# A two-layer encoder trunk on one core: the second layer's compressed rows normalised and turned for all token tiles together

## The chip, the cores and the metric

The kernel runs on one core of a Trainium2 chip. The metric is the device time of one execution in microseconds (us); the median of several runs is given. A core has five engines with a queue of instructions each: TensorE (PE in the profile, with its weight loads as PEld), VectorE (DVE), ScalarE (ACT), GpSimd (POOL) and SyncE (SP), which here issues the DMAs. Each engine works through its queue in order; semaphores make it wait for others.

## The reference

Two layers over 512 tokens of width 1024, in float32. Layer 0 is neighbourhood attention; layer 1, which the change touches, is multi-head latent attention with 16 heads:

```python
def mixer_mla(xn, w_in, q_norm, w_qb, kv_norm, w_kvb, w_out):
    c_q, c_kv, k_rope, z = jnp.split(xn @ w_in, [384, 384 + 256, 384 + 256 + 32], axis=-1)
    q = (rmsnorm(c_q, q_norm) @ w_qb).reshape(B, S, H, 64 + 32)
    q_nope, q_pe = jnp.split(q, [64], axis=-1);  q_pe = apply_rope(q_pe, cos, sin)
    kv = (rmsnorm(c_kv, kv_norm) @ w_kvb).reshape(B, S, H, 64 + 64)
    k_nope, v = jnp.split(kv, [64], axis=-1)
    k_pe = apply_rope(k_rope[:, :, None, :], cos, sin)      # one rotary key for all heads
    k = concat([k_nope, broadcast(k_pe)]);  q = concat([q_nope, q_pe])
    o = block_attention(q, k, v)                            # dense, softmax over 512 keys
    return (o.reshape(B, S, H * 64) * silu(z)) @ w_out
```

Each layer ends with an output projection, a residual add and a gated per-layer embedding; one RMS norm closes the trunk.

## The kernel before

Tokens lie in four tiles of 128 (NT = 4). Every float32 operand of a matmul is split into a rounded part (hi) and its remainder (lo), and a product is made of three matmuls: hi by hi, lo by hi, hi by lo. `load_w` (line 67) fetches a weight tile by a DMA on SP, ACT makes hi (line 76) and POOL makes lo (line 77); three buffers each. `split` (line 81) does the same for a result in PSUM: ACT copies hi (line 83), DVE subtracts (line 85, or 87 with a scale). `mms` (line 93) issues a chain of matmuls (line 96). PSUM has eight banks: two named mm, two named S, three named T for transposes and one named O.

The order of each engine's queue is not the order of the program's lines. The kernel is built with a planner that keeps a model of the engines' time: among the instructions that it holds ready, it takes the earliest in program order, and so lays out every queue ahead. `issue_after(ins)` adds that what is traced inside it on the engine of `ins` comes after `ins` in that engine's queue.

Layer 1, up to the attention, is done in these steps:

- **Compression (`mla_c`, line 408).** The 672 columns c_q (384), c_kv (256) and the rotary key (32) are computed in two parts, of 384 and of 288 columns. In each part all four token tiles take 24 matmuls (names ps_mm and ps_S), and ACT copies the result into the tile's own rows `c` (line 423). Then, tile by tile: `rms` of c_q and c_kv into one buffer `cn` of 768 columns (ACT squares with a sum, line 104; DVE forms the mean, line 105; POOL takes the power -1/2, line 106; DVE scales, line 111); the rotary key by four products (lines 436 to 439) into `tp` and sums (lines 441, 442) into two places of `cn`, whose other columns are cleared (lines 434, 435); six transposes (line 122), of which five blocks are split into `cT` and the sixth into the slabs `slab_h` and `slab_l`.
- **Rotary rows.** Two sets of query and key tiles (`sets`: qe, qo, ke, ko, hi and lo each) serve the head pairs in turn. Twelve DMAs (`move`, line 90) take the rotary key's rows from the slabs to ke, ko and, as zeros, to qo of both sets.
- **Heads (`mla_heads`).** `z_phase` computes seven of eight gates z (24 matmuls each, activation in line 152). `group(g)` (line 477), for four heads, computes the rotary queries (ACT copy, line 483; a shuffle and products, lines 484 to 487; hi and lo, lines 490 and 491) and then the values: for each token tile six matmuls into 256 columns of an mm bank, which `v_split` (line 174) splits into a tile `vt`. `project(j)` (line 507), for a pair of heads, computes queries and keys into two mm banks, splits the halves into the set of j, and moves the rotary queries by four DMAs. `attend(j)` (line 527) runs two heads (`mla_head`): for each of four query tiles three score matmuls into a bank S, a row maximum (DVE, line 559), the exponential with a sum (ACT, line 561), a division (DVE and POOL, lines 562 and 563), four transposes and a split; then eight matmuls into O.

```python
        zs = self.z_phase(a["mla_z"], xT, range(NEARLY))
        group(0)
        last = project(0)
        zs.update(self.z_phase(a["mla_z"], xT, range(NEARLY, 8)))
        for j in range(8):
            if j < 7 and j % 2 == 1:
                group((j + 1) // 2)
            attend(j)
            if j < 7:
                last = project(j + 1)
```

Of the kernel before, what the change touches and what calls it, by code (L numbers as in the profile page):

```python
# [13 lines left out]
F32 = mybir.dt.float32  # L14
F32R = mybir.dt.float32r
AF = mybir.ActivationFunctionType
# [3 lines left out]
P = 128  # L20
# [12 lines left out]
def win(t, r0, r1, off, dims):  # L33

    b = t[r0:r1]
    return bass.AP(tensor=b.tensor, offset=b.offset + off, ap=[list(b.ap[0])] + [list(d) for d in dims])


class Trunk:
# [52 lines left out]
    def mms(self, out, terms):  # L92
        nc = self.nc
        n = len(terms)
        for i, (l, r) in enumerate(terms):
            last = nc.tensor.matmul(out, l, r, start=i == 0, stop=i == n - 1)  # L96
        return last
# [76 lines left out]
    def v_split(self, vt, ps):  # L174

        src = ps.rearrange("p (g e c) -> p g e c", g=2, e=2)
        hi = win(vt, 0, P, 0, [[256, 2], [192, 2], [1, 64]])
        lo = win(vt, 0, P, 64, [[256, 2], [64, 2], [1, 64]])
        self.split(hi, lo, src)
# [228 lines left out]
    def mla_c(self, pool, xT, cT, sets):  # L408
# [5 lines left out]
        cs = [pool.tile([P, 672], F32, name=f"c{t}", tag="c", bufs=4) for t in range(NT)]  # L414
        xh, xl = xT
        L = lambda s, k, t: s[k // 4][:, k % 4, t * P:(t + 1) * P]
        for part, (w0, wn) in enumerate(((0, 384), (384, 288))):
            ws = [self.load_w(a["mla_c"][part][c], 2 * wn, extra=c == 3) for c in range(4)]
            for t in range(NT):
                ps = self.psum("S" if part == 0 and t >= 2 else "mm")  # L420
                W = lambda s, k: ws[k // 2][s][:, (k % 2) * wn:(k % 2 + 1) * wn]
                self.mms(ps[:, :wn], self.by_chunk(lambda s, k: L(xT[s], k, t), W))
                nc.scalar.activation(cs[t][:, w0:w0 + wn], ps[:, :wn], AF.Copy)
        slab_h = pool.tile([P, S], F32R, name="slab_h", tag="slab", bufs=2)
        slab_l = pool.tile([P, S], F32R, name="slab_l", tag="slab", bufs=2)
        for t in range(NT):
            c = cs[t]
            cn = pool.tile([P, 768], F32, name="cn", tag="cn", bufs=1)
            self.rms(cn[:, 0:384], c[:, 0:384], gq, 384)
            self.rms(cn[:, 384:640], c[:, 384:640], gkv, 256)  # L430
            cos, sin = tok[:, t, 0, :], tok[:, t, 1, :]
            x1, x2 = c[:, 640:656], c[:, 656:672]
            tp = pool.tile([P, 64], F32, name="tp", tag="tp", bufs=2)
            nc.vector.memset(cn[:, 640:672], 0.0)
            nc.vector.memset(cn[:, 736:768], 0.0)
            nc.vector.tensor_tensor(out=tp[:, 0:16], in0=x1, in1=cos, op=ALU.mult)
            nc.vector.tensor_tensor(out=tp[:, 16:32], in0=x2, in1=sin, op=ALU.mult)
            nc.vector.tensor_tensor(out=tp[:, 32:48], in0=x1, in1=sin, op=ALU.mult)
            nc.vector.tensor_tensor(out=tp[:, 48:64], in0=x2, in1=cos, op=ALU.mult)
            for b in (672, 704):  # L440
                nc.vector.tensor_tensor(out=cn[:, b:b + 16], in0=tp[:, 0:16], in1=tp[:, 16:32], op=ALU.subtract)
                nc.vector.tensor_tensor(out=cn[:, b + 16:b + 32], in0=tp[:, 32:48], in1=tp[:, 48:64], op=ALU.add)
            t1 = self.transposes([cn[:, i * P:(i + 1) * P] for i in range(4)])
            self.split(cT[0][:, 0:4, t * P:(t + 1) * P], cT[1][:, 0:4, t * P:(t + 1) * P],
                       t1.rearrange("p (a b) -> p a b", a=4))
            t2 = self.transposes([cn[:, i * P:(i + 1) * P] for i in range(4, 6)])
            self.split(cT[0][:, 4, t * P:(t + 1) * P], cT[1][:, 4, t * P:(t + 1) * P], t2[:, 0:P])
            self.split(slab_h[:, t * P:(t + 1) * P], slab_l[:, t * P:(t + 1) * P], t2[:, P:2 * P])
        for st in sets:
            for s, sl in enumerate((slab_h, slab_l)):  # L450
                self.move(st["ke"][s][64:96], sl[64:96])
                self.move(st["ko"][s][0:64], sl[0:64])
                self.move(st["qo"][s][0:32], sl[0:32])

    def mla_heads(self, pool, xT, cT, sets, oT):
# [21 lines left out]
        def group(g):  # L477
# [293 lines left out]
```

## Time and profile before

| | |
|---|---|
| median of 3 runs | 690.96 us (690.71 to 692.72) |
| the profiled execution's own time | 690.26 us |
| its span, first to last instruction | 688.5 us |
| TensorE's granted clock | 0.998 |
| busy: PE, PEld, DVE, ACT, POOL | 664.4, 566.9, 356.3, 402.1, 396.7 us |
| HBM traffic over the span | 107 GB/s |

A row of the profile names the line of the kernel, the engine, the operation, and the tiles as out<-in, then shapes, count and times. In a timeline a row begins with its start and its length in us; neighbours of one kind are merged (x8 is eight of them), and brackets give the engine's idle time just before and what ended it. The lengths of neighbouring matmuls overlap. In the table by stretches each engine has its busy time in that stretch. The rows of a tile give the least, the middle and the greatest length in ns.

### The profile page before, as it was taken

Reading aid. Unit: us, or ns where it says so; the run is one execution under the profiler, and the core shown is the slowest. Engines: PE = TensorE matmul, PEld = TensorE weight load, DVE = VectorE, ACT = ScalarE, POOL = GpSimd, SP = SyncE. Lnnn points to the kernel's source line nnn. Section 1 sums busy time; section 2 is a strip of 40 time slices with the busy share of each in tenths; the row PEclk is TensorE's granted clock in tenths of the full one; section 3 lists DMA queues with packets and bytes.
Section 4 is the critical chain, followed back from the end, with each engine's and each line's share of the span. In section 5 each row is a group of like instructions: output and inputs, shape, how many; then the busy total and the mean of one; then the engine's idle time right before and its main releaser. Section 6 shows DMA issues by size and latency. Waiting matters only on the chain.

```text
span 688.5 us, 10118 instructions
## 1 busy us (share of the span) xinstructions
PE 664.4 (97%) x3580; PEld 566.9 (82%) x3580; DVE 356.3 (52%) x813; ACT 402.1 (58%) x799; POOL 396.7 (58%) x309
## 2 busy tenths in 40 slices
PE   5999999999999999999999998999999999999995
PEld 4789898998988888788899886787888777887885
DVE  4300364647737624633524503788988886055333
ACT  6722576666767562643443634878888878426433
POOL 1753557467575565853044634777789867658511
PEclk9999999999999999999999999999999999999999
DMA  8731423323223127544243344203121201584122
GB/s 324 234 121 62 133 86 104 105 72 97 85 92 108 40 97 301 167 130 135 89 104 107 107 121 116 81 23 93 24 70 37 86 1 68 191 308 154 61 77 92
DMA packets 28642, 77.53 MB, mean 113 GB/s; under 512 B 3632, under 2 KB 6704, under 8 KB 28592
## 3 DMA queue, kind: packets, MB, share of 16 engines
q1 hardware_dynamic: 28592, 76.89, 33.9%
q8 instruction: 28, 0.46, 0.3%
q14 instruction: 22, 0.18, 0.1%
HBM read 65.34 MB, written 8.39 MB: 107 GB/s over the span
## 4 chain that ended last, share of the span: by engine, by line
PE 86%; ACT 5%; DVE 4%; issue 2%; DMA 1%; POOL 1%; SPq 0%; POOLq 0%; DVEq 0%; ACTq 0%
PE ps_mm L96 63%; PE ps_S L96 9%; PE ps_T L122 5%; PE ps_O L96 4%; PE ps_O L335 2%; PE ps_T L323 1%; ACT ex L561 1%; ACT whi L76 1%; DMA x<-x 1%; PE ps_S L288 1%; PE ps_S L287 1%; DVE mx L559 1%; POOL wlo L77 0%; DVE mx L301 0%; ACT pt_hi L83 0%
## 5 line engine op out<-in xcount | busy, mean ns | idle before, releaser
L77 POOL TENSOR_TENSOR wlo<-wraw,whi 128x1024 fp32r<-128x1024 f32 (+3 forms) x96 | 218.3, 2287 | 118.5 <-ACT whi L76 68.4
L76 ACT ACTIVATE whi<-wraw 128x1024 fp32r<-128x1024 f32 (+4 forms) x100 | 97.9, 988 | 97.0 <-PE ps_mm L96 32.1
L563 POOL TENSOR_TENSOR ex<-ex,rc 128x512 f32<-128x512 f32 x64 | 66.2, 1048 | 20.7 <-DVE rc L562 13.9
L96 PE MATMUL ps_mm<-whi,hnT 128*128 128x512 f32 (+1 forms) x272 | 69.7, 377 | 0.0
L96 PEld LDWEIGHTS ps_mm<-whi,hnT 128*128 128x128 f32 x272 | 49.5, 188 | 9.5
L310 POOL TENSOR_TENSOR ex<-ex,rc 128x128 f32<-128x128 f32 (+1 forms) x64 | 34.3, 560 | 38.1 <-DVE rc L306 36.5
L559 DVE TENSOR_REDUCE mx<-ps_S 128x1 f32<-128x512 f32 x64 | 43.7, 685 | 15.3 <-PE ps_S L96 14.3
L96 PE MATMUL ps_mm<-xh,whi 128*128 128x512 f32 x192 | 50.9, 398 | 0.1
L96 PE MATMUL ps_mm<-xh,wlo 128*128 128x512 f32 x192 | 49.1, 391 | 0.0
L561 ACT ACTIVATE ex<-ps_S,mx 128x512 f32<-128x512 f32 x64 | 44.1, 689 | 8.2 <-DVE mx L559 6.7
L96 PE MATMUL ps_mm<-xl,whi 128*128 128x512 f32 x192 | 48.6, 392 | 0.0
L85 DVE TENSOR_TENSOR pt_lo<-ps_T,pt_hi 128x512 fp32r<-128x512 f32 x64 | 43.0, 679 | 5.0 <-ACT pt_hi L83 4.6
L305 ACT ACTIVATE ex<-ex,mx 128x128 f32<-128x128 f32 (+1 forms) x64 | 30.2, 473 | 22.0 <-DVE mx L301 21.6
L106 POOL TENSOR_TENSOR rs<-ss,half 128x1 f32<-128x1 f32 x24 | 13.0, 549 | 50.3 <-DVE ss L105 49.0
L96 PEld LDWEIGHTS ps_mm<-xl,whi 128*128 128x128 f32 x192 | 35.6, 188 | 7.3
L96 PEld LDWEIGHTS ps_mm<-xh,wlo 128*128 128x128 f32 x192 | 35.6, 188 | 7.0
L83 ACT ACTIVATE pt_hi<-ps_T 128x512 fp32r<-128x512 f32 x64 | 37.0, 597 | 7.6 <-PE ps_T L122 7.3
L96 PE MATMUL ps_mm<-wlo,hnT 128*128 128x512 f32 (+1 forms) x136 | 40.6, 379 | 0.0
L96 PEld LDWEIGHTS ps_mm<-xh,whi 128*128 128x128 f32 x192 | 34.5, 188 | 6.4 <-ACT z L152 0.4
L122 PE MATMUL ps_T<-ident,ex 128*128 128x128 f32 x256 | 36.3, 273 | 0.2 <-DVE pt_lo L85 0.2
L122 PEld LDWEIGHTS ps_T<-ident,ex 128*128 128x128 f32 x256 | 30.7, 141 | 6.8 <-issue 0.7
L85 DVE TENSOR_TENSOR vt<-ps_mm,vt 128x256 fp32r<-128x256 f32 x32 | 13.2, 415 | 44.3 <-ACT vt L83 44.0
(215 smaller groups left out, 1579.7 us busy)
## 6 DMA issues: line engine op xcount, KB each, us to landing
pe<-pe SPq DMA_DIRECT2D x32, 256.0 KB, 2.9
wraw<-na_qk SPq DMA_DIRECT2D x16, 512.0 KB, 3.4
wraw<-gate SPq DMA_DIRECT2D x16, 512.0 KB, 3.4
wraw<-na_z SPq DMA_DIRECT2D x8, 512.0 KB, 4.2
wraw<-na_v SPq DMA_DIRECT2D x8, 512.0 KB, 3.3
wraw<-na_o SPq DMA_DIRECT2D x8, 512.0 KB, 3.4
wraw<-mla_z SPq DMA_DIRECT2D x8, 512.0 KB, 4.2
wraw<-mla_o SPq DMA_DIRECT2D x8, 512.0 KB, 3.6
```

Source lines behind the costliest of these rows:

```text
L76: nc.scalar.activation(hi[:, c], raw[:, c], AF.Copy)
L77: (rest or nc.gpsimd).tensor_tensor(out=lo[:, c], in0=raw[:, c], in1=hi[:, c].bitcast(F32), op=ALU.subtract)
L83: nc.scalar.activation(hi, src, AF.Copy, scale=scale)
L85: nc.vector.tensor_tensor(out=lo, in0=src, in1=hi.bitcast(F32), op=ALU.subtract)
L96: last = nc.tensor.matmul(out, l, r, start=i == 0, stop=i == n - 1)
L122: self.nc.tensor.transpose(t[:, i * P:(i + 1) * P], b, self.ident)
L305: self.last_exp = nc.scalar.activation(e, e, AF.Exp, bias=mx[:, qt:qt + 1], accum_out=sm[:, qt:qt + 1])
L310: nc.gpsimd.tensor_tensor(out=e, in0=e, in1=rc[:, qt:qt + 1].to_broadcast([P, e.shape[1]]), op=ALU.mult)
L335: nc.tensor.matmul(O[:, o:o + w], vh[kt], s[:, c:c + w], start=n == 0, stop=n == 7, skip_group_check=True)
L559: nc.vector.reduce_max(mx[:, c], sp, axis=AX.X, negate=True)
L561: nc.scalar.activation(ex, sp, AF.Exp, bias=mx[:, c], accum_out=sm[:, c])
L563: nc.gpsimd.tensor_tensor(out=ex, in0=ex, in1=rc[:, c].to_broadcast([P, S]), op=ALU.mult)
```

## The change

- In `mla_c` the four tiles' rows are one buffer `c` of 128 x 4 x 672. The squares are taken by ACT straight from PSUM, behind the copy, with the sums in one tile `ss` of eight columns. POOL forms mean and power for four tiles at once, in each part; DVE scales the rows in place. The rotary key of all four tiles is computed in eight wide instructions into a cleared tile `kr`. The transposes of all tiles come behind that.
- Only the first set gets its rotary rows from the slabs (six DMAs). The second set's six are copied from the first set, traced after `project(0)`.
- In `group` two token tiles share one mm bank: twelve matmuls, and one split of 512 columns into a `vt` of twice the width.
- `mms` notes its last matmul, and `attend(0)` is traced under `issue_after` of the eighth gate's last matmul.

```diff
@@ -411,46 +412,50 @@
         nc.sync.dma_start(tok, a["rope_tok"])
         gq = self.bcast(pool, a["q_norm"], 384, "gq")
         gkv = self.bcast(pool, a["kv_norm"], 256, "gkv")
-        cs = [pool.tile([P, 672], F32, name=f"c{t}", tag="c", bufs=4) for t in range(NT)]
+        c = pool.tile([P, NT, 672], F32, name="c", tag="c", bufs=1)
+        ss = pool.tile([P, 2 * NT], F32, name="ssc", tag="ssc", bufs=1)
         xh, xl = xT
         L = lambda s, k, t: s[k // 4][:, k % 4, t * P:(t + 1) * P]
-        for part, (w0, wn) in enumerate(((0, 384), (384, 288))):
-            ws = [self.load_w(a["mla_c"][part][c], 2 * wn, extra=c == 3) for c in range(4)]
+
+        for part, (w0, wn, n, g) in enumerate(((0, 384, 384, gq), (384, 288, 256, gkv))):
+            ws = [self.load_w(a["mla_c"][part][k], 2 * wn, extra=k == 3) for k in range(4)]
             for t in range(NT):
                 ps = self.psum("S" if part == 0 and t >= 2 else "mm")
                 W = lambda s, k: ws[k // 2][s][:, (k % 2) * wn:(k % 2 + 1) * wn]
                 self.mms(ps[:, :wn], self.by_chunk(lambda s, k: L(xT[s], k, t), W))
-                nc.scalar.activation(cs[t][:, w0:w0 + wn], ps[:, :wn], AF.Copy)
+                nc.scalar.activation(c[:, t, w0:w0 + wn], ps[:, :wn], AF.Copy)
+                sq = pool.tile([P, 384], F32, name="sqc", tag="sqc", bufs=1)
+                nc.scalar.activation(sq[:, :n], ps[:, :n], AF.Square, accum_out=ss[:, part * NT + t:part * NT + t + 1])
+            r = ss[:, part * NT:(part + 1) * NT]
+            nc.gpsimd.tensor_scalar(r, r, 1.0 / n, EPS, op0=ALU.mult, op1=ALU.add)
+            nc.gpsimd.tensor_tensor(out=r, in0=r, in1=self.half.to_broadcast([P, NT]), op=ALU.pow)
+            for t in range(NT):
+                v = c[:, t, w0:w0 + n]
+                nc.vector.scalar_tensor_tensor(v, v, ss[:, part * NT + t:part * NT + t + 1], g, op0=ALU.mult, op1=ALU.mult)
+
+        kr = pool.tile([P, NT, P], F32, name="kr", tag="kr", bufs=1)
+        nc.gpsimd.memset(kr, 0.0)
+        tp = pool.tile([P, 4, NT, 16], F32, name="tp", tag="tp", bufs=1)
+        x1, x2 = c[:, :, 640:656], c[:, :, 656:672]
+        cos, sin = tok[:, :, 0, :], tok[:, :, 1, :]
+        for i, (x, f) in enumerate(((x1, cos), (x2, sin), (x1, sin), (x2, cos))):
+            nc.vector.tensor_tensor(out=tp[:, i], in0=x, in1=f, op=ALU.mult)
+        for b in (32, 64):
+            nc.vector.tensor_tensor(out=kr[:, :, b:b + 16], in0=tp[:, 0], in1=tp[:, 1], op=ALU.subtract)
+            nc.vector.tensor_tensor(out=kr[:, :, b + 16:b + 32], in0=tp[:, 2], in1=tp[:, 3], op=ALU.add)
         slab_h = pool.tile([P, S], F32R, name="slab_h", tag="slab", bufs=2)
         slab_l = pool.tile([P, S], F32R, name="slab_l", tag="slab", bufs=2)
         for t in range(NT):
-            c = cs[t]
-            cn = pool.tile([P, 768], F32, name="cn", tag="cn", bufs=1)
-            self.rms(cn[:, 0:384], c[:, 0:384], gq, 384)
-            self.rms(cn[:, 384:640], c[:, 384:640], gkv, 256)
-            cos, sin = tok[:, t, 0, :], tok[:, t, 1, :]
-            x1, x2 = c[:, 640:656], c[:, 656:672]
-            tp = pool.tile([P, 64], F32, name="tp", tag="tp", bufs=2)
-            nc.vector.memset(cn[:, 640:672], 0.0)
-            nc.vector.memset(cn[:, 736:768], 0.0)
-            nc.vector.tensor_tensor(out=tp[:, 0:16], in0=x1, in1=cos, op=ALU.mult)
-            nc.vector.tensor_tensor(out=tp[:, 16:32], in0=x2, in1=sin, op=ALU.mult)
-            nc.vector.tensor_tensor(out=tp[:, 32:48], in0=x1, in1=sin, op=ALU.mult)
-            nc.vector.tensor_tensor(out=tp[:, 48:64], in0=x2, in1=cos, op=ALU.mult)
-            for b in (672, 704):
-                nc.vector.tensor_tensor(out=cn[:, b:b + 16], in0=tp[:, 0:16], in1=tp[:, 16:32], op=ALU.subtract)
-                nc.vector.tensor_tensor(out=cn[:, b + 16:b + 32], in0=tp[:, 32:48], in1=tp[:, 48:64], op=ALU.add)
-            t1 = self.transposes([cn[:, i * P:(i + 1) * P] for i in range(4)])
+            t1 = self.transposes([c[:, t, i * P:(i + 1) * P] for i in range(4)])
             self.split(cT[0][:, 0:4, t * P:(t + 1) * P], cT[1][:, 0:4, t * P:(t + 1) * P],
                        t1.rearrange("p (a b) -> p a b", a=4))
-            t2 = self.transposes([cn[:, i * P:(i + 1) * P] for i in range(4, 6)])
+            t2 = self.transposes([c[:, t, 4 * P:5 * P], kr[:, t, :]])
             self.split(cT[0][:, 4, t * P:(t + 1) * P], cT[1][:, 4, t * P:(t + 1) * P], t2[:, 0:P])
             self.split(slab_h[:, t * P:(t + 1) * P], slab_l[:, t * P:(t + 1) * P], t2[:, P:2 * P])
-        for st in sets:
-            for s, sl in enumerate((slab_h, slab_l)):
-                self.move(st["ke"][s][64:96], sl[64:96])
-                self.move(st["ko"][s][0:64], sl[0:64])
-                self.move(st["qo"][s][0:32], sl[0:32])
+        for s, sl in enumerate((slab_h, slab_l)):
+            self.move(sets[0]["ke"][s][64:96], sl[64:96])
+            self.move(sets[0]["ko"][s][0:64], sl[0:64])
+            self.move(sets[0]["qo"][s][0:32], sl[0:32])
 
     def mla_heads(self, pool, xT, cT, sets, oT):
         nc, a = self.nc, self.a
@@ -492,15 +497,17 @@
             R[g] = rh, rl
             wkv = self.load_w(a["mla_kv"][g], 1024)
             vts = []
-            for t in range(NT):
+            for t0 in range(0, NT, 2):
                 ps = self.psum("mm")
-                L = lambda s, k: cT[s][:, 3 + k, t * P:(t + 1) * P]
                 W = lambda s, k: wkv[s][:, 512 + k * 256:512 + (k + 1) * 256]
-                self.mms(ps[:, :256], [(L(0, k), W(0, k)) for k in range(2)] + [(L(1, k), W(0, k)) for k in range(2)]
-                         + [(L(0, k), W(1, k)) for k in range(2)])
-                vt = pool.tile([P, S], F32R, name="vt", tag="vt", bufs=8)
-                self.v_split(vt, ps[:, :256])
-                vts.append(vt)
+                for t in (t0, t0 + 1):
+                    L = lambda s, k: cT[s][:, 3 + k, t * P:(t + 1) * P]
+                    self.mms(ps[:, (t - t0) * 256:(t - t0 + 1) * 256],
+                             [(L(0, k), W(0, k)) for k in range(2)] + [(L(1, k), W(0, k)) for k in range(2)]
+                             + [(L(0, k), W(1, k)) for k in range(2)])
+                vt = pool.tile([P, 2 * S], F32R, name="vt", tag="vt", bufs=4)
+                self.v_split(vt, ps)
+                vts += [vt[:, :S], vt[:, S:]]
             V[g] = vts
             W_[g] = wkv, self.load_w(a["mla_qn"][g], 768)
 
@@ -535,11 +542,16 @@
         zs = self.z_phase(a["mla_z"], xT, range(NEARLY))
         group(0)
         last = project(0)
+        for s in range(2):
+            for n, r in (("ke", slice(64, 96)), ("ko", slice(0, 64)), ("qo", slice(0, 32))):
+                self.move(sets[1][n][s][r], sets[0][n][s][r])
         zs.update(self.z_phase(a["mla_z"], xT, range(NEARLY, 8)))
+        first = self.last_mm.ins
         for j in range(8):
             if j < 7 and j % 2 == 1:
                 group((j + 1) // 2)
-            attend(j)
+            with self.tc.issue_after(first) if j == 0 else nullcontext():
+                attend(j)
             if j < 7:
                 last = project(j + 1)
         return last.ins
```

`v_split` takes the number of groups of 128 columns from the shape of its bank (`g = ps.shape[1] // 128`) where it had 2.

More of the change, by code (lines that the diff above doesn't have):

```diff
@@ L95, in mms @@
         for i, (l, r) in enumerate(terms):
-            last = nc.tensor.matmul(out, l, r, start=i == 0, stop=i == n - 1)
+            last = self.last_mm = nc.tensor.matmul(out, l, r, start=i == 0, stop=i == n - 1)
         return last
@@ L174, in v_split @@
     def v_split(self, vt, ps):
-        src = ps.rearrange("p (g e c) -> p g e c", g=2, e=2)
-        hi = win(vt, 0, P, 0, [[256, 2], [192, 2], [1, 64]])
-        lo = win(vt, 0, P, 64, [[256, 2], [64, 2], [1, 64]])
+        g = ps.shape[1] // 128
+        src = ps.rearrange("p (g e c) -> p g e c", g=g, e=2)
+        hi = win(vt, 0, P, 0, [[256, g], [192, 2], [1, 64]])
+        lo = win(vt, 0, P, 64, [[256, g], [64, 2], [1, 64]])
         self.split(hi, lo, src)
```

## The prediction

> **What bounds the kernel now.** I read the page first: its engine line and the chain of waits by engine.
>
> ```profile
> span 688.5 us, 10118 instructions
> PE 664.4 (97%) x3580; PEld 566.9 (82%) x3580; DVE 356.3 (52%) x813; ACT 402.1 (58%) x799; POOL 396.7 (58%) x309
> ...
> PE 86%; ACT 5%; DVE 4%; issue 2%; DMA 1%; POOL 1%; SPq 0%; POOLq 0%; DVEq 0%; ACTq 0%
> ```
>
> TensorE (PE) is busy 664.4 of 688.5 us and owns 86% of the chain. The diff adds and removes no matmul and no transpose: the value products keep their 24 matmuls per group, the 24 turns of compressed rows stay 24. So the time can move only through PE's idle time, 24.1 us in all, and only through that part of it that lies where the edits act. The table by stretches (columns: PE, PEld, DVE, ACT, POOL busy with counts, clock, DMA) and the list of what PE waited for between 340 and 480 us show how little that is:
>
> ```profile
> 350.00:360.00 10.00, 9.42 (x56) 8.85 (x55) 1.29 (x2) 5.69 (x11) 7.09 (x5) 1.00 0.40 109
> 410.00:420.00 10.00, 8.79 (x48) 7.31 (x47) 3.15 (x6) 4.03 (x7) 6.26 (x5) 1.00 0.74 215
> 420.00:430.00 10.00, 9.23 (x39) 6.75 (x38) 3.11 (x5) 3.78 (x7) 2.42 (x2) 1.00 0.25 68
> 430.00:440.00 10.00, 8.68 (x42) 6.96 (x41) 5.35 (x11) 8.68 (x17) 6.68 (x5) 1.00 0.15 34
> ```
>
> ```profile
> PE ps_S L96 <- ACT ex L561: 2.5, 2, 1.3
> PE ps_mm L96 <- DVE vt L85: 0.8, 1, 0.8
> PE ps_S L96 <- ACT ke L83: 0.7, 1, 0.7
> PE ps_mm L96 <- ACT c L423: 0.6, 1, 0.6
> PE ps_mm L96 <- ACT xr L483: 0.3, 1, 0.3
> ```
>
> 0.58 us is idle at the seam of the two compression parts (350 to 360), 1.21, 0.77 and 1.32 us between 410 and 440, where the first value products, the first head pair's projection and the eighth gate lie. The five waits add to 4.9 us. That is the stake: well under 1% of the span.
>
> **Squares from PSUM.** Rows of ACT and PE at the seam, and the squares of now:
>
> ```profile
> 358.77 0.85 ACT L423 ACTIVATE c<-ps_mm 128x384 f32<-128x384 f32 x2
> ...
> 359.30 0.53 PE L96 MATMUL ps_mm<-whi,x1h 128*128 128x288 f32 x2 [0.58 <-ACT c L423]
> ...
> L104 ACT ACTIVATE cn<-c x8: 417/477/536, 359.9 to 393.7; 128x384 f32<-128x384 f32 x4, 128x256 f32<-128x256 f32 x4
> L104 ACT ACTIVATION_READ_ACCUMULATOR cn<-c x8: 187/204/212, 360.3 to 394.0; 128x1 f32 x8
> ```
>
> Part two's first matmul waits 0.58 us for a bank that the copy of c empties. The eight squares stay eight, but now they read the bank too, so it is held for one more ACT instruction and its accumulator read: at most 0.54 + 0.20 us, less what the two overlap by. I take +0.5 us. The ends are 0 (the other tile's bank is freed first) and +1.1 (both copies of 0.42 us and a square go ahead of the release). At the other tiles 24 matmuls lie between a bank's uses, and nothing waits.
>
> **Normalising and turning together.** Eight powers on POOL become two (each with a small multiply-add that DVE did eight times), and a clearing of 512 columns is added there; on DVE 32 rope instructions of 16 columns become eight of 64 (strided, over the four tiles), and eight clearings go. The eight scalings stay, in place. All of part two's work now starts behind the last compressed tile. What covers it is the gate phase (z):
>
> ```profile
> 372.69 2.10 PE L96 MATMUL ps_mm<-x1h,whi 128*128 128x512 f32 x8
> ...
> 412.96 1.52 PE L96 MATMUL ps_mm<-cT,whi 128*128 128x512 f32 x6
> ```
>
> From 372.69 to 412.96 us PE runs seven gates without a wait, and the first reader of the turned rows comes behind them. So I cost this edit at 0, as PE's order is written ahead and can put the 24 turns anywhere in those 40 us. What it costs if a turn stands too early is a rival below.
>
> **Six of twelve moves later.** On SP's queue:
>
> ```profile
> 402.30 0.60 SPq L90 DMA_DIRECT2D ke<-slab_h  x1
> ...
> 409.99 0.53 SPq L75 DMA_DIRECT2D wraw<-mla_z  x1
> ...
> 421.84 0.51 SPq L90 DMA_DIRECT2D qe<-rh  x1
> ...
> 414.57 1.06 ACT L76 ACTIVATE whi<-wraw 128x1024 fp32r<-128x1024 f32 x1 [0.81 <-PE ps_mm L96]
> ```
>
> The twelve moves hold SP from 402.30 us to the fetch of the eighth gate's weights at 409.99, 0.64 us each. Six fewer would fetch these 3.8 us earlier, but ACT's conversion of them waits for PE, not for the transfer, so nothing is won. The six later copies take the same 3.8 us of SP. They are traced past the four rope moves of the first pair and ahead of the eighth gate's load. That load is traced behind the rope moves now as well, and the queue has it 12 us ahead of them (409.99 against 421.84), since it waits for nothing; the copies' source rows, too, are long in place by then. So both can go early, and the copies at worst put the load back to where it is now. Cost 0; the upper end, a load held back by some copies until its conversion is late, is +1.
>
> **Values, two tiles to a bank.**
>
> ```profile
> 416.16 0.74 PE L96 MATMUL ps_mm<-whi,cT 128*128 128x256 f32 x4 [0.29 <-ACT xr L483]
> ...
> 419.03 0.74 PE L96 MATMUL ps_mm<-whi,cT 128*128 128x256 f32 x4 [0.79 <-DVE vt L85]
> ...
> 417.12 1.52 DVE L485 TENSOR_TENSOR xr<-xr,rope_c 128x512 f32<-128x512 f32 x1
> ...
> L83 ACT ACTIVATE vt<-ps_mm x32: 360/383/410, 56.9 to 529.1; 128x256 fp32r<-128x256 f32 x32
> ```
>
> Now four banks are asked for, of two. Tile two waits 0.29 us for the bank of the rotary queries, tile four 0.79 us, since the rest of tile two stood on DVE behind a rotary product that took 1.52 us. With two tiles to a bank both waits lie inside a bank: the first pair keeps PE busy until the rotary bank is free, and the second pair takes that one. I take -1.1 us, the two waits. The ends are -1.2 (all idle time of that stretch) and -0.4: the rest of pair one can fall behind the same 1.52 us, and then the query projection waits for it.
>
> **The eighth gate ahead of the first scores.**
>
> ```profile
> 422.81 0.61 PE L96 MATMUL ps_mm<-cT,wlo 128*128 128x512 f32 x2
> 424.10 1.45 PE L96 MATMUL ps_S<-ke,qe 96*128 96x512 f32 x4 [0.68 <-ACT ke L83]
> 425.64 2.06 PE L96 MATMUL ps_mm<-x1h,whi 128*128 128x512 f32 x8
> ...
> 438.83 0.96 PE L96 MATMUL ps_S<-ko,qo 128*128 128x512 f32 x3 [1.32 <-ACT ex L561]
> ...
> 424.80 0.69 DVE L87 SCALAR_TENSOR_TENSOR qo<-ps_mm,qo 64x512 fp32r<-64x512 f32 x1
> ...
> 431.98 1.28 ACT L561 ACT_TABLE_LOAD   x1
> ```
>
> The projection ends at 423.42 us. Four score matmuls of the first head stand next, behind a wait of 0.68; the eighth gate starts at 425.64, just after DVE's last read of its bank (424.80 + 0.69). The change puts every PE instruction of the first attention behind the gate. The gate's bank comes free no sooner, so the whole 2.2 us from 423.42 to 425.64 become idle. The four scores then run behind the gate, some 1.0 us (eight matmuls of that width take 2.06), where PE now waits 1.32 us for the exponentials. Those hang on ACT, whose table load stands behind the gate's own activation, so they come no later. What is lost ahead of the gate is won behind it: net 0. The ends are +1.0 (the exponentials slip with the scores) and -0.6 (see the first rival).
>
> **Later groups.** Three more groups empty two banks of 512 columns instead of four of 256: 4 x 0.383 us on ACT against, by the length of the copies in the compression rows (0.42 for 384), some 2 x 0.60. That frees 0.3 us per group on an engine that PE waits for. I take -0.5 us in all; since every queue behind 413 us is laid out anew, the ends are -2 and +2.
>
> **Sum:** +0.5 + 0 + 0 - 1.1 + 0 - 0.5 = -1.1 us, or 689.2 against the profiled execution's 690.26 us (its span of 688.5 plus 1.8 around it). That execution lies 0.7 under the median, so the forecast in medians is 690.96 - 1.1 = 689.9 us.
>
> **Rivals.** *More falls away than those waits.* The row that ends the z bank's life is delayed because ACT takes the first half of the keys between the two halves of the queries:
>
> ```profile
> 422.10 0.59 ACT L83 ACTIVATE qe<-ps_mm 64x512 fp32r<-64x512 f32 x1 [0.29 <-PE ps_mm L96]
> 423.46 0.59 ACT L83 ACTIVATE ke<-ps_mm 64x512 fp32r<-64x512 f32 x1 [0.77 <-PE ps_mm L96]
> ...
> 468.85 0.96 PE L96 MATMUL ps_S<-ke,qe 96*128 96x512 f32 x3 [1.16 <-ACT ex L561]
> ```
>
> With the scores held back the keys are no longer urgent; should the queries go first, the gate starts 0.6 us sooner. If also the square is hidden (0.5 less) and the wait of 1.16 at 468.85 goes in the new layout, the sum is -1.1 - 0.6 - 0.5 - 1.2 = -3.4, 687.6 us. For it speaks that all three are waits on order and not on work; against it, that a new layout can just as well bring waits of its own.
>
> *The turns stand too early.* Where POOL and DVE meet:
>
> ```profile
> 371.16 7.18 POOL L77 TENSOR_TENSOR wlo<-wraw,whi 128x1024 fp32r<-128x1024 f32 x3 [5.62 <-ACT whi L76]
> ...
> L441 DVE TENSOR_TENSOR cn<-tp x8: 138/169/2382, 364.5 to 392.9; 128x16 f32<-128x16 f32 x8
> L111 DVE SCALAR_TENSOR_TENSOR cn<-c,rs,gkv x4: 475/478/484, 365.6 to 395.3; 128x256 f32<-128x256 f32 x4
> ...
> 380.69 0.47 DVE L111 SCALAR_TENSOR_TENSOR cn<-c,rs,gkv 128x256 f32<-128x256 f32 x1
> ...
> 383.71 0.82 PE L122 MATMUL ps_T<-ident,cn 128*128 128x128 f32 x6
> ```
>
> Three weight remainders run on POOL without a break just when part two ends, and a DVE product of 16 columns, usually 0.17 us, took 2.38 us among them, about one remainder's length. Tile two's rows were ready at 381.16 and its turns stood at 383.71: 2.5 us of room. Now all four scalings of part two and eight rope instructions want DVE in that stretch. If three of them lose 2.2 us each, the turns come 6.6 us late, 4.1 more than the room, and PE waits that long: -1.1 + 4.1 = +3.0, 694.0 us. It decides from 2.5 us of lateness, and the kernel is slower by more than 0.3% from 5.7. Against it: the scalings themselves never took over 0.484 us, and the rope work can go ahead while the powers are awaited. The Trainium skill, "SBUF — State Buffer", section "Who interferes with whom", says that a VectorE instruction with two SBUF inputs blocks against a GpSimd instruction that reads SBUF, and that whichever issues first keeps the pair of ports to its end. The trace agrees with 2.38 us; by that rule every scaling of the batch may be held, and the sum would be this rival's.
>
> *The edits do nothing that shows:* all waits covered or replaced, 691.
>
> **How the numbers follow.** 0.3%, 2.1 us, is about what a measurement of this kernel can tell from no change. The forecast has 0.38, with a range of its own from 688.4 to 691.8; the first rival 0.36; the second 0.24; nothing at all 0.02. Faster by over 0.3% (under 688.9) are the first rival and 0.04 of the forecast: 0.40. Within 0.3% are 0.33 of the forecast and the 0.02: 0.35. Slower: 0.24 and 0.01 of the forecast: 0.25. The range from 686.8 to 693.6 leaves out the far end of each rival, about 0.1 on each side.
>
> **What would show it.** Right: PE busy within 1 us of 664; a wait of about 1 us at the seam; no wait for vt; turns in a bunch between 375 and 395 us with no idle time before them; an idle stretch of about 2 us ahead of the eighth gate, and less than 1 us where PE waited 1.32 for ex. Wrong: PE idle before a ps_T of c, or new waits for ex or pt_hi in the attention past 440 us that add to over 2 us.

## The result, and the profile after

The changed kernel takes 696.97 us (median of four, 696.17 to 698.17); the kernel before, on the same chip, 691.68 (690.71 to 692.72). The ratio is 1.0078, 95% interval 1.0053 to 1.0103: slower by 5.3 us. The forecast of 689.9 was wrong in sign, and the time lies above the range. The profiled execution took 698.17 us, so it stands 1.2 over the median.

Page of the kernel after: span, engine line, chain by engine.

```profile
span 696.4 us, 10055 instructions
PE 668.9 (96%) x3580; PEld 569.6 (82%) x3580; DVE 349.3 (50%) x765; ACT 401.8 (58%) x791; POOL 394.7 (57%) x306
PE 84%; ACT 6%; DVE 4%; issue 2%; POOL 2%; DMA 2%; SPq 0%; POOLq 0%; DVEq 0%; ACTq 0%
```

The matmuls are the same 3580, yet PE's busy time rose by 4.5 us (664.4 before). DVE and POOL have less to do, and the kernel is slower: their time was not on the path. What PE waited for between 340 and 480 us, and the table by stretches:

```profile
PE ps_mm L96 <- DVE qo L87: 2.2, 1, 2.2
PE ps_mm L96 <- DVE vt L85: 1.3, 1, 1.3
PE ps_mm L96 <- ACT sqc L428: 1.2, 1, 1.2
PE ps_T L122 <- DVE pt_lo L85: 0.8, 1, 0.8
PE ps_T L122 <- POOL ex L575: 0.6, 1, 0.6
PE ps_S L96 <- ACT ex L573: 0.4, 1, 0.4
```

```profile
350.00:360.00 10.00, 9.13 (x55) 8.56 (x53) 1.29 (x2) 5.17 (x9) 6.58 (x5) 1.00 0.33 107
420.00:430.00 10.00, 7.44 (x27) 5.77 (x28) 3.57 (x6) 2.89 (x5) 3.37 (x3) 0.88 0.41 108
430.00:440.00 10.00, 10.00 (x45) 8.15 (x44) 3.27 (x7) 6.85 (x12) 4.43 (x4) 0.95 0.21 57
470.00:480.00 10.00, 9.33 (x42) 7.43 (x43) 7.31 (x15) 7.10 (x16) 6.31 (x7) 0.83 0.31 103
```

The six waits add to 6.5 us where five added to 4.9. And the clock column, 1.00 in all stretches that the prediction showed, now reads 0.88, 0.95 and 0.83: (0.12 + 0.05) x 10 = 1.7 us of clock are missing from 420 to 440, and 1.7 from 470 to 480. These 3.4 us are most of the 4.5 us by which the busy time grew.

**The eighth gate, after.** PE's timeline (start, length, then the group; in brackets the idle time before it):

```profile
423.42 0.61 PE L96 MATMUL ps_mm<-cT,wlo 128*128 128x512 f32 x2
426.25 2.54 PE L96 MATMUL ps_mm<-x1h,whi 128*128 128x512 f32 x8 [2.22 <-DVE qo L87]
428.59 3.15 PE L96 MATMUL ps_mm<-x1l,whi 128*128 128x512 f32 x8
431.58 2.00 PE L96 MATMUL ps_mm<-x1h,wlo 128*128 128x512 f32 x8
...
441.08 0.96 PE L96 MATMUL ps_S<-ko,qo 128*128 128x512 f32 x3 [0.42 <-ACT ex L573]
```

The 2.2 us idle ahead of the gate and the shorter wait behind it (0.42 for 1.32) are as forecast. Not forecast: the gate's first sixteen matmuls take 2.54 and 3.15 us instead of 2.0, with the clock at half for a part of them.

**The values, after.** DVE's and PE's rows:

```profile
417.97 1.71 DVE L490 TENSOR_TENSOR xr<-xr,rope_c 128x512 f32<-128x512 f32 x1
419.61 1.27 DVE L85 TENSOR_TENSOR vt<-ps_mm,vt 128x512 fp32r<-128x512 f32 x2
```

```profile
418.66 0.40 PE L96 MATMUL ps_mm<-wlo,cT 128*128 128x256 f32 x2
420.34 1.66 PE L96 MATMUL ps_mm<-cT,whi 128*128 128x512 f32 x6 [1.28 <-DVE vt L85]
```

All 24 value matmuls run without a wait, and then the query projection waits 1.28 us for the first pair's rest, which stands on DVE behind the 1.71 us product: the worse end that the prediction named for this edit.

### The profile page after: what moved, and what is told of

It is laid out like the page before. It is cut to its first block, busy times and chain, and to the rows that moved or that the text cites. A ratio compares the mean times of both kernels' runs of the same rounds, so it can differ in the third digit from the quotient of the medians.

```text
span 696.4 us, 10055 instructions
## 1 busy us (share of the span) xinstructions
PE 668.9 (96%) x3580; PEld 569.6 (82%) x3580; DVE 349.3 (50%) x765; ACT 401.8 (58%) x791; POOL 394.7 (57%) x306
## 4 chain that ended last, share of the span: by engine, by line
PE 84%; ACT 6%; DVE 4%; issue 2%; POOL 2%; DMA 2%; SPq 0%; POOLq 0%; DVEq 0%; ACTq 0%
PE ps_mm L96 63%; PE ps_S L96 7%; PE ps_T L122 5%; PE ps_O L96 4%; PE ps_O L336 2%; PE ps_T L324 1%; ACT ex L573 1%; DMA x<-x 1%; ACT pt_hi L83 1%; PE ps_S L289 1%; PE ps_S L288 1%; POOL wlo L77 1%; DVE mx L571 1%; ACT whi L76 1%; DMA wraw<-mla_c 0%
## 5 line engine op out<-in xcount | busy, mean ns | idle before, releaser
L85 DVE TENSOR_TENSOR vt<-ps_mm,vt 128x256 fp32r<-128x256 f32 (+1 forms) x24 | 12.1, 508 | 43.4 <-ACT vt L83 43.1
L106 POOL TENSOR_TENSOR rs<-ss,half 128x1 f32<-128x1 f32 x16 | 8.8, 551 | 42.8 <-DVE ss L105 42.8
```

Of the source, the lines that this page charges most:

```text
L85: nc.vector.tensor_tensor(out=lo, in0=src, in1=hi.bitcast(F32), op=ALU.subtract)
```

## The experiments

Each time stands beside runs of the kernel before on the same chip.

### The parts of the change, one by one

Four kernels show which part holds the loss: the normalising and the moves alone and the values alone (their code as in the diff of the change), `issue_after` alone (the edit below), and the change without it.

> The kernel before with the compressed rows normalised and turned together and the second set's rotary rows copied later; values and order of the eighth gate as before. In the changed kernel PE waited 1.17 us at the seam of the compression parts instead of 0.58, for the square that reads the bank. Theory A (the loss sits in the attention, laid out anew because of the values' pairing and the eighth gate's place): only the seam is paid, +0.5 us, 0 to +1 against before, and PE's waits past 440 us are those of before. Theory B (the later, bunched turns and copies disturb what follows): +2.5 us or more, with new waits past 410 us.

> The kernel before with two value tiles to a bank, nothing else changed. Theory A1 (the pairing of values is what disturbs the attention): +3 us or more against before, PE waiting for pt_hi, pt_lo or ex past 440 us for over 4 us in sum. Theory A2 (the eighth gate's place does it): -0.5 us, -1.1 to +0.5, the two waits between 415 and 420 us gone and one for vt of about 1.3 us ahead of the query projection left.

```diff
+        first = self.last_mm.ins
...
-            attend(j)
+            with self.tc.issue_after(first) if j == 0 else nullcontext():
+                attend(j)
```

> The kernel before with the first attention's PE work held behind the eighth gate, nothing else changed. Theory A2 (the empty stretch of 2.2 us ahead of the gate and the layout that follows cost most): +2 to +4 us, an empty stretch of about 2.2 us and, in part of the executions, TensorE granted half its clock for 3.4 us behind it (+1.7 us more). Theory A1: within 1 us of before, since what is lost ahead of the gate is won behind it.

> The changed kernel without the hold on the first attention: its scores may run ahead of the eighth gate again. Theory A2: 2 to 4 us faster than the changed kernel, so +1 to +3 against before. Theory A1: as slow as the changed kernel, +4 to +6 against before.

| kernel | median | before | ratio, 95% interval |
|---|---|---|---|
| normalising and moves | 691.55 | 691.67 | 0.9998, 0.9989 to 1.0007 |
| values | 696.62 | 691.67 | 1.0066, 1.0052 to 1.0080 |
| `issue_after` | 693.44 | 691.67 | 1.0028, 1.0017 to 1.0039 |
| the change without `issue_after` | 696.73 | 691.67 | 1.0076, 1.0063 to 1.0089 |

The values alone bring nearly the whole loss (+4.9), and PE's waits for exponentials past 440 us come to 5.3 us, as theory A1 said. `issue_after` alone costs 1.8, more than A1 and a little less than A2 gave it; leaving it out of the change wins nothing, which A1 said: with paired values the first scores wait anyway. PE's row in the change without it:

```profile
425.61 1.17 PE L96 MATMUL ps_S<-ke,qe 96*128 96x512 f32 x4 [1.85 <-DMA qe<-rh]
```

The rotary queries' DMA comes later, and 1.85 us stand idle ahead of the scores instead of 2.22 ahead of the gate.

A part of the 4.9 us is the clock. By their mean clock, the five executions of the values alone took 695.02 us at 0.997, 695.85 and 696.62 at 0.995, 697.14 and 697.94 at 0.993. The profiled one, of 697.94 us, has the half clock twice: from 427 us, and from 550 us, behind a wait of 1.27 us for an exponential:

```profile
550.00:560.00 10.00, 10.00 (x48) 8.18 (x47) 6.51 (x13) 5.87 (x14) 6.23 (x7) 0.83 0.16 54
```

### Which value groups

Both kernels use the wide `vt` in all groups, as the change does. The first pairs banks in group 0 only, the second in the three others.

```diff
+                if g == 0:      # in the second kernel: if g > 0
                     ps = self.psum("mm")
...
+                else:
+                    vt = pool.tile([P, 2 * S], F32R, name="vt", tag="vt", bufs=4)
+                    for t in (t0, t0 + 1):
+                        ps = self.psum("mm")
...
+                        self.v_split(vt[:, (t - t0) * S:(t - t0 + 1) * S], ps[:, :256])
```

> The kernel before with two value tiles to a bank in the first group of heads alone; the three later groups take a bank for each tile, into halves of the same wide tile. Theory T (pairing in the later groups sends the filling matmuls ahead of the attention, so that the stretch behind the last of them holds more work and more waits): the order of the attention stays that of before, 691 to 693 us, 0 to +1.5 against before for the wait for vt of 1.5 us and the empty stretch ahead of the first scores. Theory F (what happens in the first group, with its empty stretch and half clock, costs all of it): +4 or more.

> The kernel before with two value tiles to a bank in the three later groups alone. Theory T: +3 to +5 us against before, and the stretch from the last filling matmul to the end of the attention 52 us instead of 47.7. Theory F: within 1 us of before.

Group 0 alone: 692.10 us against 691.33, ratio 1.0010 (0.9997 to 1.0023), no difference that shows. The later groups alone: 694.66, ratio 1.0051 (1.0036 to 1.0066), +3.3 us; the three of its six executions at a mean clock of 0.998 took 693.76 to 694.95 us, so at most a few tenths of that are the half clock. So most of the loss lies in the three groups that are computed beside the attention. What PE waits for from 430 to 596 us, before and with the later groups paired:

```profile
PE ps_S L96 <- ACT ex L561: 2.9, 4, 1.3
PE ps_O L96 <- ACT pt_hi L83: 0.7, 1, 0.7
...
PE ps_T L122 <- DVE pt_lo L85: 0.2, 1, 0.2
```

```profile
PE ps_S L96 <- ACT ex L575: 5.4, 9, 1.3
...
```

The waits for `vt` are not among them. PE waits nine times instead of four until an exponential on ACT empties a score bank. One such place, near 550 us (PE's, then ACT's rows):

```profile
547.33 0.97 PE L96 MATMUL ps_S<-ke,qe 96*128 96x512 f32 x3 [1.28 <-ACT ex L575]
548.13 0.39 PE L96 MATMUL ps_mm<-whi 128*128 128x512 f32 x1
...
550.67 0.39 PE L96 MATMUL ps_mm<-wlo,whi 128*128 128x512 f32 x1
```

```profile
551.54 0.60 ACT L83 ACTIVATE pt_hi<-ps_T 128x512 fp32r<-128x512 f32 x1 [2.04 <-PE ps_T L122]
```

First PE stands for ACT; then PE runs twelve matmuls of the per-layer embedding, work meant to fill gaps, and ACT stands 2.04 us for the transposes queued behind them. Both engines have work, in an order that does not fit.

### The eighth gate's bank

What the gate waited for was an mm bank. Here `z_phase` takes a bank S for it (with and without `issue_after`, and in the whole change):

```diff
-            ps = self.psum("mm")
+            ps = self.psum(bank)
...
-        zs.update(self.z_phase(a["mla_z"], xT, range(NEARLY, 8)))
+        zs.update(self.z_phase(a["mla_z"], xT, range(NEARLY, 8), bank="S"))
```

> The kernel with the first attention held behind the eighth gate (the pairing and the rest as before), and the eighth gate's sums in a bank S instead of mm. Theory G (the hold costs because the gate waits 2.2 us for the queries' bank, and because PE's clock is halved behind that empty stretch in part of the executions): the wait is gone, -2 us against before, -3 to -1, and no half clock between 425 and 435 us. Rival (the hold costs by the order it gives to the attention): +1 to +2, as without the other bank.

> The whole changed kernel with the eighth gate's sums in a bank S. Theory G: 2 to 4 us faster than the changed kernel (2.2 of empty stretch, and the half clock in part of the executions), so +1 to +3 against before; what is left is the stretch behind the last filling matmul. Rival: no faster than the changed kernel, +5.

> The kernel before with the eighth gate's sums in a bank S and nothing else; the first scores are not held. If the bank is what wins: -2 us against before, as with the hold. If the hold is needed beside it: -1 to +0.5.

On the kernel before with `issue_after`: 689.44 us against 691.33, ratio 0.9970 (0.9958 to 0.9982). Without `issue_after`: 689.25 against 691.41, 0.9971 (0.9960 to 0.9983). The whole change with it: 694.37, 1.0033 (1.0019 to 1.0046). So the bank is worth 2 us against the kernel before, 4 against the kernel with `issue_after` alone (693.44) and 2.6 in the change, and the order written by `issue_after` is worth nothing with it. PE's rows (bank S and `issue_after`):

```profile
416.21 2.08 PE L96 MATMUL ps_S<-x1h,whi 128*128 128x512 f32 x8
...
421.38 2.00 PE L96 MATMUL ps_S<-x1h,wlo 128*128 128x512 f32 x8
...
426.90 0.61 PE L96 MATMUL ps_mm<-cT,wlo 128*128 128x512 f32 x2
428.20 1.92 PE L96 MATMUL ps_S<-ke,qe 96*128 96x512 f32 x6 [0.68 <-ACT ke L83]
```

The gate now runs from 416 us between the value products, in the stretch where PE waited for `xr` and `vt`; the stall of 2.2 us is gone, and so is the half clock.

### Why the later groups cost 3.3 us

*Theory one: the fill runs out.* Counted in PE's queue at the usual pitch of each width (0.227 us for 512 columns, 0.109 for 128), 44.6 us of matmuls stand behind the end of the last projection, up to the last row into O, when the later groups are paired; before, 43.4. There only the embedding's 41 matmuls, 9.3 us of both numbers, are left to fill gaps. `issue_after` holds the last projection back, so that as little stands behind it as before; the second kernel does the same, further on, to the kernel with the gate in bank S:

```diff
+                with self.tc.issue_after(self.turned[42]) if j == 6 else nullcontext():
-                last = project(j + 1)
+                    last = project(j + 1)
...
+            self.turned.append(self.last_tr.ins)     # last transpose of each query tile of each head
```

(45 in place of 42 in the second kernel)

> Pairing in the three later groups, as in the run that cost 0.5%, but the last projection's matmuls are held on PE behind the transposes of the eleventh head's third query tile, so that as much filling work as before the change is left beside the last heads (43.4 us of matmuls behind the last filling one, as before, where the pairing alone leaves 44.5). Theory T (the end of the attention without filling work is what the pairing lengthens): 2 to 3.5 us come back, 0 to +1.5 against before, and the stretch behind the last filling matmul takes 47 to 48.5 us. Rival (the pairing costs by banks held longer in the groups themselves): +3 as without the hold.

> The version with the gate in bank S and the scores held, and the last projection held behind the twelfth head's second query tile: 31 us of matmuls instead of 43.4 are left behind the last filling one. Theory T taken further: the waits of 3.5 us in the stretch without filling work shrink by 1 to 2 us, -1 to -2 beyond the same kernel without this hold (-3 to -4 against before). Rival (the filling work is then missing ahead of it): no gain, -2 to 0 against before, with new waits between 530 and 550 us.

694.05 us against 691.41, ratio 1.0043 (1.0030 to 1.0055): of 3.3 us only some 0.7 came back, which the two intervals don't tell from nothing. The tail did shrink, from 542.11 (the last projecting row) to 592.56 (the last row into O) without the hold, to 544.31 to 592.23 with it, 2.5 us less, but the stretch before grew, with a new wait just behind the held projection:

```profile
544.31 0.61 PE L96 MATMUL ps_mm<-cT,wlo 128*128 128x512 f32 x2
...
547.76 1.82 PE L122 MATMUL ps_T<-ident,ex 128*128 128x128 f32 x12 [1.47 <-DVE pt_lo L85]
```

The second kernel took 690.61, ratio 0.9989 (0.9980 to 0.9998), 1.2 us more than without the hold (689.44): the last row into O starts 3.1 us sooner (584.02 for 587.14), but from there to the end of the span it takes 4.0 us more (104.1 for 100.1), as the embedding's matmuls that no longer fit beside the attention come behind it. Theory one fell as the sole cause.

*Theory two: every paired group pays; its rival: the order of the whole attention is laid out anew, and what comes out is uneven.* One later group paired at a time (`if g == 1`, 2, 3), and the three groups paired but each bank emptied in two halves:

```diff
-                    self.v_split(vt, ps)
+                    for i in range(2):
+                        self.v_split(vt[:, i * S:(i + 1) * S], ps[:, i * 256:(i + 1) * 256])
```

> Paired banks in the second group alone; the other groups as before. Theory 'price of a pair' (a bank of 512 columns comes free later, and every paired group pays for it): a third of the 3.3 us of groups two to four, +1.1 us, in each of these three kernels. Theory 'new order' (pairing as such costs nothing; the queues of the whole attention are laid out anew, and what comes out is uneven): the three single groups differ by over 1 us among themselves and do not add to 3.3 us; one of them lies within 0.7 us of before.

> Paired banks in the third group alone. Theory 'price of a pair': +1.1 us. Theory 'new order': any amount from -0.7 to +3, another one than for the second group.

> Paired banks in the fourth group alone, the only one of the three whose order leaves 44.6 us of matmuls instead of 43.4 behind the last filling matmul. Theory 'price of a pair': +1.1 us. Theory 'new order': the group with the largest amount, +1.2 us or more, for that tail.

> Paired banks in groups two to four, but each emptied in two halves of 256 columns, so that no copy or subtraction is longer than before. Theory 'price of a pair', if it is the length of the instructions of 512 columns: the time of before, within 0.7 us. The same theory, if it is the bank held for twelve matmuls: +3.3 us as with whole banks. Theory 'new order': an amount of its own between 0 and +4 us, since the order differs from both; PE's idle time again spread over the attention and not ahead of the value matmuls.

| paired | median (before 691.43) | ratio, 95% interval |
|---|---|---|
| second group | 691.60 | 1.0001, 0.9992 to 1.0010 |
| third group | 693.97 | 1.0037, 1.0024 to 1.0050 |
| fourth group | 693.94 | 1.0044, 1.0030 to 1.0059 |
| three groups, emptied in halves | 692.78 | 1.0017, 1.0005 to 1.0028 |

The same edit costs nothing, 2.5 and 2.5 us, together 5.2 where the three at once cost 3.3. A price per pair would be even and would add up; it is neither. The third group also speaks against theory one: its order leaves 43.4 us of matmuls at the end, as before, and costs as much as the fourth, which leaves 44.6. Emptied in halves the loss is 1.35 us, between the two figures that a price per pair gave (within 0.7, or 3.3); a part of the price may still be the long instructions, since this order differs from both, and this kernel doesn't decide it. What PE waits for from 430 to 596 us, third group, fourth group, halves:

```profile
PE ps_S L96 <- ACT ex L575: 3.3, 5, 1.3
PE ps_mm L96 <- DVE qo L87: 1.5, 1, 1.5
PE ps_O L96 <- ACT pt_hi L83: 0.5, 1, 0.5
...
```

```profile
PE ps_S L96 <- ACT ex L575: 4.5, 8, 1.3
PE ps_mm L96 <- DVE qo L87: 0.5, 1, 0.5
...
```

```profile
PE ps_S L96 <- ACT ex L576: 1.5, 2, 1.3
PE ps_T L122 <- DVE pt_lo L85: 1.5, 1, 1.5
PE ps_O L96 <- ACT pt_hi L83: 0.5, 1, 0.5
...
```

Each has other waits at other places, none at the values themselves. One of them, the third group's 1.5 us, is for an mm bank, the kind of wait that a longer-held bank could make; with all three groups paired it isn't there. Listed waits in the attention come to 3.8 us before, 5.4 with the three paired, 5.6 and 5.2 with the third and fourth, 3.9 with halves: they rise with the times, but by only about half of the loss or less. The rest is in gaps too short to be listed. That shows when PE's matmuls are counted that start from 430 to 597 us: before, 444 of 512 columns; with the three groups paired 431, with the second alone 442, with the third 432, with the fourth 432, with halves 440. All other kinds are there in the same number in each. At 0.227 us apiece the missing ones are 3.0, 0.5, 2.7, 2.7 and 0.9 us, beside 3.3, 0.2, 2.5, 2.5 and 1.35 measured. So the loss of each of these kernels is PE coming late inside the attention, and little of it lies elsewhere.

### The best of the parts

The normalising and the moves of the change, `issue_after`, the gate in bank S, the squares from the copied rows instead of from PSUM, the values as before:

```diff
-                nc.scalar.activation(sq[:, :n], ps[:, :n], AF.Square, accum_out=ss[:, part * NT + t:part * NT + t + 1])
+                nc.scalar.activation(sq[:, :n], c[:, t, w0:w0 + n], AF.Square, accum_out=ss[:, part * NT + t:part * NT + t + 1])
```

> The changed kernel without the pairing of values, with the eighth gate's sums in a bank S and the squares taken from the copied rows instead of the bank. All of the change but the pairing, with its two new waits mended: -2 us against before, -3 to -1, with a wait at the seam of 0.6 us (0.58 before). If the normalising of all tiles together has a cost that the seam's wait hid: -1 to 0.

689.01 us against 691.41, ratio 0.9967 (0.9955 to 0.9978): faster than both kernels. The bank alone brought 689.25, and 689.44 with `issue_after`, so it is the bank that does it.

## Why the prediction was wrong, point by point

- **Later groups (-0.5, ends -2 and +2).** The step that failed. Alone it measured +3.3 us, beyond its upper end. Its mechanism was true and beside the point. ACT's rows for the values in the attention, before and with paired banks:

```profile
L83 ACT ACTIVATE vt<-ps_mm 128x256 fp32r<-128x256 f32 x12 | 4.7, 390 | 0.8 <-PE ps_mm L96 0.5
```

```profile
L83 ACT ACTIVATE vt<-ps_mm 128x512 fp32r<-128x512 f32 x6 | 3.6, 600 | 2.7 <-PE ps_mm L96 2.2 <-PE ps_O L96 0.5
```

  The 1.1 us of ACT that the step counted (0.3 per group) were freed. But PE waits for single exponentials, not for ACT's sum: it stood four times for one before and nine times with the later groups paired, and started thirteen matmuls fewer in the attention's 167 us. "Laid out anew" stood in the text as a reason for a symmetric end of 2 us; it should have been a mechanism of its own with more room on the bad side, for the order of before already left only 3.8 us of listed waits in the attention: little to win, much to lose. Why this order fits worse is shown only as far as the places. That there is no fixed price per pair follows from the uneven single groups; that it is the order, and not a pair's bank or its longer instructions that hurt in one place and not in another, is not shown. Which decision of the planner does it was not tried.
- **The eighth gate (net 0, ends -0.6 and +1.0).** The stall of 2.2 us and the shorter wait behind it are there, but `issue_after` alone cost 1.8. Of eight executions of that kernel the three at a mean clock of 0.996 or more took 692.29 to 693.11 us, the five at 0.993 or 0.994 692.91 to 694.72: at the high clock the median is 692.41, 0.7 us over the kernel before, which the ends allowed for, and the rest is the half clock, a term that the sum did not have. Where the 0.7 us arise is not shown.
- **Values, group 0 (-1.1, ends -1.2 and -0.4).** Measured +0.8, not to be told from 0. In the change the two waits went as said (in group 0 alone the one for `xr` stayed, at 0.62 us), and the projection's wait of 1.28 came as named. In group 0 alone, in all groups alone and in the change without `issue_after` one more came unforeseen, for the rotary queries' DMA: its source, the copy to `rh`, now stands on ACT behind the query's first half (in group 0 alone at 423.43 behind 422.94 us; before at 421.18, ahead of 422.10), and PE waits 1.9 us for it. The end of -0.4 was too good.
- **Squares from PSUM (+0.5, ends 0 and +1.1).** Right: ACT's and PE's rows at the seam:

```profile
360.05 0.20 ACT L428 ACTIVATION_READ_ACCUMULATOR sqc<-ps_mm 128x1 f32 x1
...
360.30 0.53 PE L96 MATMUL ps_mm<-whi,x1h 128*128 128x288 f32 x2 [1.17 <-ACT sqc L428]
```

  0.58 became 1.17 us: the square and its read stand before the release. (With the normalising and the moves alone it is 0.91.)
- **Normalising and turning together, moves (0 and 0).** Right: 691.55 against 691.67 for both with the seam. The turns stood at 387.80 us and later without a wait. The gate's load moved up to 407.00 (409.99 before); of the six copies one went ahead of the rotary moves and three stood among them, from 426.39 us, with nobody waiting.
- **The rival "more falls away"** had the gate 0.6 us sooner; it started 0.6 later (426.25 against 425.64). Its 687.6 is near what the gate's own bank brought by another way.
- **The rival "turns too early"** said slower, but not for what came. The holding on DVE is there, and larger than supposed, yet PE did not wait for it:

```profile
374.25 5.19 DVE L442 TENSOR_TENSOR tp<-c,tok 128x64 f32<-128x64 f32 x4 [7.53 <-ACT c L426]
379.36 0.34 DVE L444 TENSOR_TENSOR kr<-tp 128x64 f32<-128x64 f32 x2
379.63 2.57 DVE L445 TENSOR_TENSOR kr<-tp 128x64 f32<-128x64 f32 x2
382.97 1.67 DVE L434 SCALAR_TENSOR_TENSOR c<-c,ssc,gkv 128x256 f32<-128x256 f32 x4 [0.77 <-POOL ssc L431]
```

  Six rotary instructions took 7.8 us beside POOL's remainders (two others 0.34). But the scalings were not held (0.42 us from one to the next), as POOL had just done the powers that release them and began its next remainder at 384.70 us, and the transposes came 3.2 us behind them. In the best of the parts one scaling did meet a remainder: POOL's began at 380.02 us and took 2.39, the scaling began at 380.08 and took 2.62 us where the other three took 0.47 to 0.49, and still PE did not wait. (The 2.38 us that the prediction called a product's are those of line 441, a difference of two products.) The rule of the Trainium skill, "SBUF — State Buffer", section "Who interferes with whom", agrees with the rotary products, and with this scaling.
- **What was to show it right or wrong.** PE's busy time left its 1 us around 664, and a wait for vt was there. The waits for ex and pt_hi past 440 us rose from 2.3 to 3.5 us, which is less than the 2 us named; with the two for pt_lo (1.1) and two for POOL's ex (1.0) the attention's come to 5.6 against 3.8. The line was drawn around two names where the loss spread over four.

Two steps failed, then: the later groups, which brought 3.3 us where -0.5 stood, and the half clock, for which the sum had no term. The parts, as far as they were measured inside the change: -0.1 (normalising, moves) + 4.9 (values in all groups, the half clock of that kernel with them) + 0.2 (`issue_after`, the change against the change without it) = 5.0 us, measured 5.3. The 1.8 us of `issue_after` alone don't belong in this sum: paired values leave PE idle at the same place anyway. Nor do the two value kernels add up to all groups, 0.8 + 3.3 = 4.1 against 4.9.

## What to carry to other kernels

Where a planner lays out all queues, an edit is not only what it adds and removes: changing a tile's shape in one stage moved waits in stages that it doesn't touch and cost 0 to 3.3 us, unevenly. So first try it in the one place that needs it, and leave the others alone. When an engine waits for a buffer, look for another buffer before changing the order: a free bank for one gate was worth 2 us with an edit of a few words, an order written by hand cost 1.8. A gap on TensorE can cost more than its length, by the slower clock behind it.

## What the runs showed of the hardware that was not expected

**Half clock behind a short gap.** PE's rows with paired values in all groups, and then in group 0 alone:

```profile
426.39 1.33 PE L96 MATMUL ps_S<-ke,qe 96*128 96x512 f32 x4 [1.90 <-DMA qe<-rh]
427.51 3.45 PE L96 MATMUL ps_mm<-x1h,whi 128*128 128x512 f32 x8
```

```profile
426.15 1.16 PE L96 MATMUL ps_S<-ke,qe 96*128 96x512 f32 x4 [1.89 <-DMA qe<-rh]
427.14 2.00 PE L96 MATMUL ps_mm<-x1h,whi 128*128 128x512 f32 x8
```

The same gap, the same matmuls: in one execution the eight of the gate run at half the clock, in the other at the full one. So the half clock can follow such a gap and need not; group 0 alone has a mean clock of 0.994 in four of its twelve executions and 0.996 to 0.998 in the others. With `issue_after` alone it came behind 2.21 us, in the kernel after behind 2.22 and again near 470 us, behind waits of 0.78 and 0.57 us with only transposes between. In the values alone and in the change without `issue_after` it came near 550 us, behind a wait of 1.27 us, where the later groups alone had 1.28 and the full clock; in the change with the gate in bank S near 468 us, behind 2.06. In all seven cases it begins 0.7 to 1.4 us after the gap, and 1.7 us of clock are missing, 3.4 us at half. In that last kernel the four executions at a mean clock of 0.998 took 692.45 to 692.65 us, the five at 0.994 to 0.996 took 694.37 to 695.27. The Trainium skill, "TensorE: Matmul & The Clock Gate", section "HAM oscillation — how this bites in real kernels", gives idle gaps over some 3.4 us as the ones to avoid; here it came behind single gaps of 1.3 to 2.2 us, and the measurement decides. That the gap is what sets it off is read from its place each time; no run lengthened or shortened a gap alone.
